# A transformer kernel whose split products read their moving columns with the two halves interleaved

## The chip, the cores and the metric

The kernel runs on one core of a Trainium2 chip. The metric is the device time of one execution in microseconds. Five engines work side by side and wait for one another by semaphores: PE multiplies matrices, DVE and ACT do elementwise work, POOL a little of it, and SP issues most transfers from the chip's main memory. PE reads both operands from the on-chip memory SBUF and adds its output into PSUM, a second on-chip memory, which DVE and ACT read ("evacuate").

## The reference

Two small transformer stacks of two layers each run one after the other over 256 tokens of width 1024, in float32. Cut to what matters:

```python
# first stack                                     # second stack
x = x + fox_mixer(rms_norm(x), ...)               x = x + gla_mixer(rmsnorm(x), ...)
x = x + square(relu(h @ w_up)) @ w_down           x = x + (silu(a) * u) @ w_down   # a, u: conv of h @ w_up
x = x + mla_mixer(h, ...)                         x = x + (b * conv(c * u)) @ w_out
x = x + square(relu(h @ w_up)) @ w_down           x = x + (silu(a) * u) @ w_down
x = rms_norm(x)                                   return rmsnorm(x)
```

The mixers are two kinds of causal softmax attention (Fox, MLA), a gated linear attention (GLA) and a short convolution. Nearly all arithmetic is in the products `h @ w` with a weight of 1024 or more rows.

## The kernel before

The tokens lie in two blocks of 128. A product of activations and weights is done in **split** form: ACT rounds a float32 operand to the format fp32r (the high part, `wh` for weights, `hh` for activations), DVE subtracts it from the original (the low part, `wl`, `hl`), and PE adds three products, high by high, high by low and low by high. In PE's terms each has a stationary operand of 128 columns, loaded anew each time, and a moving one whose columns stream through. In the trace a product reads `out<-moving,stationary`.

There are four kinds of split product. `proj` and `accum` hold an activation block and move 512 weight columns (384 or 320 in MLA); `mm3` issues the three. `proj_T` holds 128 weight columns and moves the activations of all 256 tokens, so its output is transposed; two such outputs share one PSUM tile. `proj_wide` moves 528 columns as twice 264. `accum_by_token` does the last products of the program token block by token block, the last ones in pieces of 256 columns. The moving columns are read in running order and land in PSUM in running order. The other products (attention scores and their use, transposes, the first two rounds of the program on unsplit data, `plain`) are ordinary float32.

Weights come by transfers into `raw` tiles (four), are split into `wh` and `wl` (five of each) and used in the order of a plan written out ahead. Output tiles are PSUM banks: four `acc`, three `up`, one `tp`. Elementwise work that follows a product is put into a queue and issued some steps later (`after`, with a table of delays, `DLY`); attention and GLA's core run as generators that put a step between the products (`side`). The order of the instructions on each engine is set when the program is built; at run time each engine takes its own in order and waits only where data is missing.

What the change touches: `mm` (line 339) issues every product; `by_row` (lines 399 and 401) multiplies a transposed output by a row of factors per token; `scaled` (line 591) multiplies by a factor per token on ACT; `scaled_wide` does so for the two tiles of `proj_wide`; `add_x` (lines 579 and 581) adds an output to x; and the evacuations of the ffn (line 616), of GLA's gate (line 1223) and of the short convolution (lines 1435 and 1447).

Of the kernel before, what the change touches and what calls it, by code (L numbers as in the profile page):

```python
# [18 lines left out]
P = 128  # L19
# [141 lines left out]
class Builder:  # L161
# [176 lines left out]
    def mm(self, out, lhsT, rhs, start, stop):  # L338
        self.nc.tensor.matmul(out, lhsT, rhs, start=start, stop=stop, skip_group_check=True)  # L339

    def mm3(self, ps, h, u, kk, n, start, stop):
        hh, hl = h
        wh, wl = u.hi[:, kk, :n], u.lo[:, kk, :n]
        self.mm(ps, hh, wh, start, False)
        self.mm(ps, hh, wl, False, False)
        self.mm(ps, hl, wh, False, stop)

    def up_tile(self):
        return self.up_p.tile([P, 512], F32, tag="up", name=self.name("up"))
# [10 lines left out]
    def proj(self, h, nk, n, evac, tiles=None, k0=0):  # L360

        ps = tiles or [self.up_tile(), self.up_tile()]
        k = k0
        while k < nk:
            u = self.unit()
            for kk in range(u.kn):
                for t in range(2):
                    self.mm3(ps[t][:, :n], h.get(t, k), u, kk, n, k == 0, k == nk - 1)
                    if k == nk - 1:
                        evac(t, ps[t])  # L370
                    self.tick()
                k += 1

    def proj_T(self, h, nk, evac, tile_fn=None):


        ps = [(tile_fn or self.up_tile)() for _ in range(2)]
        k = 0
        while k < nk:
            u = self.unit()  # L380
            for kk in range(u.kn):
                hh, hl = h.both(k)
                for f in range(4):
                    o = ps[f // 2][:, f % 2 * S:f % 2 * S + S]
                    wh, wl = [x[:, kk, f * P:(f + 1) * P] for x in (u.hi, u.lo)]
                    self.mm(o, wh, hh, k == 0 and f % 2 == 0, False)
                    self.mm(o, wl, hh, False, False)
                    self.mm(o, wh, hl, False, k == nk - 1)
                    if f % 2:
                        if k == nk - 1:  # L390
                            evac(f // 2, ps[f // 2])
                        self.tick()
                k += 1

    def by_row(self, out, ps, row, mul=None):

        r = lambda x: x.rearrange("p (i s) -> p i s", i=2)
        if mul is None:
            self.nc.vector.tensor_tensor(out=r(out), in0=r(ps), in1=row, op=ALU.mult)
        else:  # L400
            self.nc.vector.scalar_tensor_tensor(out=r(out), in0=r(ps), scalar=mul, in1=row, op0=ALU.mult, op1=ALU.mult)  # L401

    def proj_wide(self, h, evac, tile_fn):

        ps = [(tile_fn(), self.acc_tile()) for _ in range(2)]
        n = WIDE // 2
        for k in range(8):
            if k % 2 == 0:
                u = self.unit()
            for t in range(2):  # L410
                hh, hl = h.get(t, k)
                for i in range(2):
                    o = ps[t][i][:, :n]
                    wh, wl = [x[:, k % 2, i * n:i * n + n] for x in (u.hi, u.lo)]
                    self.mm(o, hh, wh, k == 0, False)
                    self.mm(o, hh, wl, False, False)
                    self.mm(o, hl, wh, False, k == 7)
                if k == 7:
                    evac(t, *ps[t])
                self.tick()  # L420

    def scaled_wide(self, out, a, b, col):

        n = WIDE // 2
        self.scaled(out[:, 0:n], a[:, 0:n], col)
        self.scaled(out[:, n:512], b[:, 0:512 - n], col)
        return b[:, 512 - n:n]

    def accum(self, acc, h, ks, first, last, done=None, cs=(0, 1)):

        for c in cs:
            k = 0
            while k < len(ks):
                u = self.unit()
                for kk in range(u.kn):
                    for t in range(2):
                        self.mm3(acc[t][c], h.get(t, ks[k]), u, kk, 512, first and k == 0, last and k == len(ks) - 1)
                        if last and k == len(ks) - 1:
                            done(t, c, acc[t][c])
                        self.tick()  # L440
                    k += 1

    def accum_by_token(self, acc, h, ks, done):

        us = [self.unit(), self.unit()]
        n = len(ks)
        xs = self.x[1][1]
        self.nc.vector.tensor_tensor(out=xs, in0=acc[1][1], in1=xs, op=ALU.add)
        for t in range(2):
            for c in range(2):  # L450
                if not (t and c):
                    for i, k in enumerate(ks):
                        self.mm3(acc[t][c], h.get(t, k), us[c], i, 512, False, i == n - 1)
                        self.tick()
                    done(t, c, acc[t][c], 0)
                    continue
                for o in (0, 256):
                    ps = self.up_tile()[:, 0:256]
                    for i, k in enumerate(ks):
                        hh, hl = h.get(t, k)  # L460
                        wh, wl = [x[:, i, o:o + 256] for x in (us[c].hi, us[c].lo)]
                        self.mm(ps, hh, wh, i == 0, False)
                        self.mm(ps, hh, wl, False, False)
                        self.mm(ps, hl, wh, False, i == n - 1)
                        self.tick()
                    done(t, c, ps, o)

    def new_acc(self):

# [103 lines left out]
    def add_x(self, hook, scale=None):  # L573
        nc = self.nc

        def done(t, c, ps, o=None):
            xs = self.x[t][c] if o is None else self.x[t][c][:, o:o + ps.shape[1]]
            if scale is None:
                nc.vector.tensor_tensor(out=xs, in0=ps, in1=xs, op=ALU.add)
            else:  # L580
                nc.vector.scalar_tensor_tensor(out=xs, in0=ps, scalar=scale[:, t:t + 1], in1=xs, op0=ALU.mult, op1=ALU.add)
            if o is None:
                hook(t, c)
            else:
                hook(t, c, xs, o)

        return done

    def scaled(self, out, ps, col):

        self.nc.scalar.activation(out=out, in_=ps, func=AF.Copy, scale=col)


# [13 lines left out]
    def ffn1(self, h, rs, hook):  # L607
# [4 lines left out]
        def evac(j):  # L612
            def f(b, ps):
                r = self.tmp_tile()
                sq = self.tmp_tile()
                nc.scalar.activation(out=r, in_=ps, func=AF.Relu)

                def square():
                    nc.vector.tensor_tensor(out=sq, in0=r, in1=r, op=ALU.mult)
                    self.after(DLY[4], lambda: self.split_pair(sq, hid, 4 * j + 2 * b))  # L620

                self.after(DLY[3], square)
            return f
# [344 lines left out]
    def mla(self, h, rs, hook):  # L968
# [20 lines left out]

        def ev_kv(t, ps):  # L990
            c = self.tmp_tile()
            self.scaled(c[:, :256], ps[:, :256], rs[:, t:t + 1])
            self.scaled(kc[:, t * 64:(t + 1) * 64], ps[:, 256:320], rs[:, t:t + 1])
            self.after(DLY[7], lambda: self.prep(c[:, :256], t, [0, 1], [(ckv, self.vec("kva"))], self.acc_tile))
            self.after(DLY[8], lambda: stat(t, c, 0, 256, 1.0 / 256))
            if t:
# [24 lines left out]

        def ev_q(t, ps):
            c = self.tmp_tile()
            self.scaled(c[:, :384], ps[:, :384], rs[:, t:t + 1])
            self.after(DLY[11], lambda: self.prep(c[:, :384], t, [0, 1, 2], [(cq, self.vec("qa"))], self.acc_tile))
            self.after(DLY[12], lambda: stat(t, c, 1, 384, 1.0 / 384))
            if t:
                self.after(DLY[12] + 6, lambda: rs2.make_row(2))
# [97 lines left out]
    def gla(self, h, rs, hook):  # L1126
# [93 lines left out]
        def ev_g(i):  # L1220
            def f(t, ps):
                gs = self.tmp_tile()
                nc.scalar.activation(out=gs, in_=ps, func=AF.Silu, scale=rs[:, t:t + 1])

                def gain():
                    nc.vector.tensor_tensor(out=gs, in0=gs, in1=hg[:, i * 512:(i + 1) * 512], op=ALU.mult)
# [195 lines left out]
    def sc(self, h, rs, hook):  # L1422
# [9 lines left out]
        def ev_u(i):  # L1432
            def f(b, ps):
                z = cs.pop(b)
                nc.vector.tensor_tensor(out=z, in0=ps, in1=z, op=ALU.mult)

                def go():
                    cv[b] = self.tmp_tile()
                    self.conv_pair(cv[b], z, cw, 4 * i + 2 * b)

                self.after(DLY[25 + b], go)
            return f

        def ev_b(i):
            def f(b, ps):
                c = cv.pop(b)
                nc.vector.tensor_tensor(out=c, in0=ps, in1=c, op=ALU.mult)
                self.after(DLY[29], lambda: self.split_pair(c, y, 4 * i + 2 * b))
            return f

# [94 lines left out]
    def start(self, h, stat):  # L1545
# [25 lines left out]
            return r  # L1571

        def plain(t, k):
            self.mm(ps[t], hg[t, 0][:, k * P:(k + 1) * P], self.raws[0][:, k], k == 0, False)

        with self.tc.manual_schedule():

# [150 lines left out]
```

## Time and profile before

| | |
|---|---|
| median of 3 runs | 1157.27 us (1157.15 to 1157.37) |
| the profiled execution's own time | 1156.24 us |
| its span, first to last instruction | 1154.5 us |
| PE busy | 1142.0 us in 7769 instructions |
| weight loads | 1030.1 us, beside PE |
| DVE busy | 804.8 us in 1196 |
| ACT busy | 610.9 us in 923 |
| mean granted TensorE clock | 0.999 |
| moved from main memory | 204.97 MB, 178 GB/s |

The page's busy share of PE says only that PE always has a product under way: products overlap, so a product that is shown with 280 ns may stand 117 ns after the one before. How fast PE runs is therefore read from the starts of products (the timeline) or from a piece of the chain of waits that holds many products in a row. Idle time stands behind a group's busy time, with what ended it.

### The profile page before, as it was taken

Reading aid. Unit: us, or ns where it says so; the run is one execution under the profiler, and the core shown is the slowest. Engines: PE = TensorE matmul, PEld = TensorE weight load, DVE = VectorE, ACT = ScalarE, POOL = GpSimd, SP = SyncE. Lnnn points to the kernel's source line nnn. Section 1 sums busy time; section 2 is a strip of 40 time slices with the busy share of each in tenths; the row PEclk is TensorE's granted clock in tenths of the full one; section 3 lists DMA queues with packets and bytes.
Section 4 is the critical chain, followed back from the end, with each engine's and each line's share of the span. In section 5 each row is a group of like instructions: output and inputs, shape, how many; then the busy total and the mean of one; then the engine's idle time right before and its main releaser. Section 6 shows DMA issues by size and latency. Waiting matters only on the chain.

```text
span 1154.5 us, 19192 instructions
## 1 busy us (share of the span) xinstructions
PE 1142.0 (99%) x7769; PEld 1030.1 (89%) x7769; DVE 804.8 (70%) x1196; ACT 610.9 (53%) x923; POOL 33.2 (3%) x55
## 2 busy tenths in 40 slices
PE   8999999999999999999999999999999999999997
PEld 6987998998888999899898789999989999999996
DVE  6686755555686755555788569777786668887775
ACT  5465554445665545444563556455555446555453
POOL 0000100000000100000010000000001000000001
PEclk9999999999999999999999999999999999999999
DMA  9744455555463556555555355556665564656551
GB/s 341 276 146 146 160 197 191 183 183 167 135 203 120 168 192 195 192 184 183 185 178 170 110 165 164 180 179 191 200 217 185 194 185 134 196 175 213 183 159 62
DMA packets 137802, 207.30 MB, mean 180 GB/s; under 512 B 10529, under 2 KB 65009, under 8 KB 137713
## 3 DMA queue, kind: packets, MB, share of 16 engines
q1 hardware_dynamic: 136576, 203.89, 55.1%
q10 hardware_dynamic: 1136, 2.17, 0.5%
q8 instruction: 61, 1.00, 0.4%
q14 instruction: 29, 0.23, 0.1%
HBM read 204.97 MB, written 1.07 MB: 178 GB/s over the span
## 4 chain that ended last, share of the span: by engine, by line
PE 92%; DVE 5%; ACT 2%; issue 1%; POOL 0%; ACTq 0%; DVEq 0%; POOLq 0%
PE up L339 52%; PE acc L339 37%; DVE wl L312 1%; PE acc L502 1%; ACT p L672 1%; DVE p L691 1%; PE tp L502 1%; ACT wh L294 0%; DVE p L682 0%; ACT junk L535 0%; PE tp L512 0%; DVE kT L1207 0%; PE acc L1582 0%; DVE pT L700 0%; DVE bias L758 0%
## 5 line engine op out<-in xcount | busy, mean ns | idle before, releaser
L312 DVE TENSOR_TENSOR wl<-raw,wh 128x1024 fp32r<-128x1024 f32 (+2 forms) x373 | 454.1, 1219 | 261.4 <-ACT wh L294 259.5
L294 ACT CAST wh<-raw 128x1024 fp32r<-128x1024 f32 (+2 forms) x373 | 389.5, 1045 | 432.3 <-PE up L339 278.2
L339 PE MATMUL up<-hh,wh 128*128 128x256 f32 x1564 | 439.2, 281 | 0.0
L339 PE MATMUL up<-hh,wl 128*128 128x256 f32 x1564 | 437.7, 280 | 0.0
L339 PE MATMUL up<-hl,wh 128*128 128x256 f32 x1564 | 436.5, 280 | 0.0
L339 PEld LDWEIGHTS up<-hh,wh 128*128 128x128 f32 x1564 | 294.3, 188 | 3.0 <-issue 1.5
L339 PEld LDWEIGHTS up<-hh,wl 128*128 128x128 f32 x1564 | 294.1, 188 | 1.5
L339 PEld LDWEIGHTS up<-hl,wh 128*128 128x128 f32 x1564 | 294.2, 188 | 0.3 <-DVE hl L491 0.2
L339 PE MATMUL acc<-wh,hh 128*128 128x512 f32 (+1 forms) x606 | 235.8, 389 | 0.2 <-DVE mx L691 0.2
L339 PE MATMUL acc<-wh,hl 128*128 128x512 f32 (+1 forms) x606 | 233.3, 385 | 0.0
L339 PE MATMUL acc<-wl,hh 128*128 128x512 f32 (+1 forms) x606 | 232.8, 384 | 0.0
L339 PEld LDWEIGHTS acc<-wh,hl 128*128 128x128 f32 x606 | 113.8, 188 | 24.5 <-DVE hl L708 0.3
L339 PEld LDWEIGHTS acc<-wh,hh 128*128 128x128 f32 x606 | 113.8, 188 | 23.1 <-DVE mx L691 0.6
L339 PEld LDWEIGHTS acc<-wl,hh 128*128 128x128 f32 x606 | 113.9, 188 | 21.6
L1340 DVE SCALAR_TENSOR_TENSOR tmp<-tmp,vecs,tmp 128x255 f32<-128x255 f32 x192 | 78.0, 479 | 18.0 <-ACT tmp L1338 18.0
L339 PE MATMUL up<-wh,hh 128*128 128x512 f32 (+4 forms) x142 | 53.9, 382 | 0.3 <-DVE tmp L401 0.3
L339 PE MATMUL up<-wl,hh 128*128 128x512 f32 (+4 forms) x142 | 51.6, 364 | 1.3 <-DVE wl L312 1.3
L339 PE MATMUL up<-wh,hl 128*128 128x512 f32 (+4 forms) x142 | 51.4, 364 | 0.0
L1338 ACT ACTIVATE tmp<-tmp,vecs 128x256 f32<-128x256 f32 x96 | 40.9, 497 | 0.0
L1349 DVE TENSOR_TENSOR hl<-tmp,hh 128x512 fp32r<-128x512 f32 x58 | 38.2, 685 | 0.0
L1348 ACT CAST hh<-tmp 128x512 fp32r<-128x512 f32 x58 | 34.2, 622 | 2.2 <-DVE tmp L1393 2.2
L339 PEld LDWEIGHTS up<-wh,hh 128*128 128x128 f32 x142 | 26.7, 188 | 7.5 <-issue 3.4
(205 smaller groups left out, 770.5 us busy)
## 6 DMA issues: line engine op xcount, KB each, us to landing
raw<-ffn_w_up SPq DMA_DIRECT2D x176, 256.0 KB, 4.1
raw<-ffn_w_up SPq DMA_DIRECT2D x32, 1024.0 KB, 5.4
raw<-ffn_w_down SPq DMA_DIRECT2D x32, 1024.0 KB, 5.0
raw<-ffn_w_down SPq DMA_DIRECT2D x44, 512.0 KB, 6.5
raw<-sc_w_in SPq DMA_DIRECT2D x12, 1024.0 KB, 5.2
raw<-fox_w_in SPq DMA_DIRECT2D x10, 1024.0 KB, 9.4
raw<-gla_w_in SPq DMA_DIRECT2D x10, 1024.0 KB, 5.1
raw<-fox_w_out SPq DMA_DIRECT2D x4, 1024.0 KB, 5.0
```

What stands on the lines that cost most here:

```text
L294: self.last_hi = nc.scalar.copy(hi[:, :kn, :w], self.raws[r][:, k:k + kn])
L312: self.last_wl = nc.vector.tensor_tensor(out=u.lo[:, :kn, :w], in0=self.raws[r][:, k:k + kn], in1=u.hi[:, :kn, :w].bitcast(F32), op=ALU.su ...
L339: self.nc.tensor.matmul(out, lhsT, rhs, start=start, stop=stop, skip_group_check=True)
L502: self.nc.tensor.transpose(tp[:, i * P:(i + 1) * P], src[:, i * P:(i + 1) * P], self.ident)
L672: self.nc.scalar.activation(out=p[:, o:o + n], in_=p[:, o:o + n], func=AF.Exp, scale=scale, bias=nm[:, j:j + 1], accum_out=sm[:, j:j + 1])
L691: self.nc.vector.tensor_tensor_reduce(out=p[:, o:o + n], in0=lgs[h][:, w], in1=bias(h)[:, w], scale=1.0, scalar=NEG, op0=ALU.add, op1=ALU. ...
L1338: nc.scalar.activation(out=out, in_=z, func=AF.Copy, scale=w[:, 2:3])
L1340: nc.vector.scalar_tensor_tensor(out=out[:, d:], in0=z[:, :S - d], scalar=w[:, 2 - d:3 - d], in1=out[:, d:], op0=ALU.mult, op1=ALU.add)
L1348: nc.scalar.copy(hi, src)
L1349: nc.vector.tensor_tensor(out=lo, in0=src, in1=hi.bitcast(F32), op=ALU.subtract)
```

## The change

A split product's moving operand is read as first column of the left half, first of the right half, second of the left, second of the right, and so on. The output is still written to PSUM in running order, so PSUM holds the columns interleaved. Each evacuation reads PSUM at every second element, the left half first and then the right, and so puts the columns back in order. `plain` shares its PSUM tiles with split products and is done the same way. [...] In MLA, the evacuation of the KV projection copies all 320 columns where it copied 256.

```diff
+    def mmw(self, out, lhsT, rhs, start, stop):
+        self.mm(out.rearrange("p (b a) -> p b a", a=2), lhsT, rhs.rearrange("p (a b) -> p b a", a=2), start, stop)
+
+    def woven(ps, n=1):
+        return ps.rearrange("p (b a) -> p a b", a=2) if n == 1 else ps.rearrange("p (i b a) -> p i a b", i=n, a=2)
+
+    def like(x, ps):
+        if len(x.shape) == 3:
+            return x.rearrange("p i (a b) -> p i a b", a=2)
+        return x.rearrange("p (a b) -> p a b", a=2) if len(ps.shape) == 3 else x.rearrange("p (i a b) -> p i a b", i=ps.shape[1], a=2)
+
     def mm3(self, ps, h, u, kk, n, start, stop):
-        self.mm(ps, hh, wh, start, False)
-        self.mm(ps, hh, wl, False, False)
-        self.mm(ps, hl, wh, False, stop)
+        self.mmw(ps, hh, wh, start, False)
+        self.mmw(ps, hh, wl, False, False)
+        self.mmw(ps, hl, wh, False, stop)
...
-                        evac(t, ps[t])
+                        evac(t, self.woven(ps[t][:, :n]))
...
-                            evac(f // 2, ps[f // 2])
+                            evac(f // 2, self.woven(ps[f // 2], 2))
...
-            self.nc.vector.tensor_tensor(out=r(out), in0=r(ps), in1=row, op=ALU.mult)
+            self.nc.vector.tensor_tensor(out=out, in0=ps, in1=row, op=ALU.mult)
         else:
-            self.nc.vector.scalar_tensor_tensor(out=r(out), in0=r(ps), scalar=mul, in1=row, op0=ALU.mult, op1=ALU.mult)
+            for i in range(2):
+                self.nc.vector.scalar_tensor_tensor(out=out[:, i], in0=ps[:, i], scalar=mul, in1=row[:, i], op0=ALU.mult, op1=ALU.mult)
...
-        self.scaled(out[:, 0:n], a[:, 0:n], col)
-        self.scaled(out[:, n:512], b[:, 0:512 - n], col)
-        return b[:, 512 - n:n]
+        m = n // 2
+        self.scaled(out[:, 0:n], a, col)
+        self.scaled(out[:, n:n + m], b[:, 0], col)
+        self.scaled(out[:, n + m:512], b[:, 1, :m - 16], col)
+        return b[:, 1, m - 16:]
...
-            self.scaled(c[:, :256], ps[:, :256], rs[:, t:t + 1])
-            self.scaled(kc[:, t * 64:(t + 1) * 64], ps[:, 256:320], rs[:, t:t + 1])
+            self.scaled(c[:, :320], ps, rs[:, t:t + 1])
+            self.scaled(kc[:, t * 64:(t + 1) * 64], ps[:, 1, 96:160], rs[:, t:t + 1])
```

On PE nothing moves but one group of four small products in GLA's core, which changes places with its neighbours; SP and POOL keep their order. Two places on ACT and DVE show what moves there. On ACT, in Fox, the evacuation of V after `proj_wide` stood as follows (`v` is the result, `acc` the output tiles, `wh` the next weights).

```order
L294 CAST wh_400<-raw_243 128x2x512
L591 ACTIVATE v_207<-acc_296,rs_117 128x264
L591 ACTIVATE v_207<-acc_297,rs_117 128x248
L591 ACTIVATE v_207<-acc_298,rs_117 128x264
L591 ACTIVATE v_207<-acc_299,rs_117 128x248
L294 CAST wh_452<-raw_253 128x2x512
```

After the change it is this.

```order
L294 CAST wh_400<-raw_243 128x2x512
L615 ACTIVATE v_207<-acc_296,rs_117 128x264
L615 ACTIVATE v_207<-acc_297,rs_117 128x132
L615 ACTIVATE v_207<-acc_297,rs_117 128x116
L615 ACTIVATE v_207<-acc_298,rs_117 128x264
L615 ACTIVATE v_207<-acc_299,rs_117 128x132
L615 ACTIVATE v_207<-acc_299,rs_117 128x116
L294 CAST wh_454<-raw_253 128x2x512
```

The two pieces of 248 columns have become two each, ahead of the next weights' rounding; GLA has the same. On DVE, in Fox's attention, a stretch with one evacuation of Q (`qT`), a step of the softmax (`nm`, `rc`) and the low part of the next weights (`wl`) was this.

```order
L401 SCALAR_TENSOR_TENSOR qT_204<-up_587,rowb_217 128x512
L769 SCALAR_TENSOR_TENSOR nm_732<-mx_727,ctok 128x4
L679 RECIPROCAL rc_761<-sm_674 128x4
L312 TENSOR_TENSOR wl_750<-raw_530,wh_749 128x2x512
L770 TENSOR_TENSOR nm_732<-nm_732,ctok 128x4
```

And it becomes this.

```order
L419 SCALAR_TENSOR_TENSOR qT_204<-up_589,rowb_217 128x256
L793 SCALAR_TENSOR_TENSOR nm_735<-mx_730,ctok 128x4
L419 SCALAR_TENSOR_TENSOR qT_204<-up_589,rowb_217 128x256
L794 TENSOR_TENSOR nm_735<-nm_735,ctok 128x4
L703 RECIPROCAL rc_765<-sm_676 128x4
L312 TENSOR_TENSOR wl_754<-raw_532,wh_753 128x2x512
```

The evacuation is in two halves with a small softmax step between them, and `nm`'s second step now stands ahead of the weights' low part; some of the rows behind, up to 30 further on, change places with their neighbours.

## Rows read from the trace of the kernel before

**Rows 1.** The page's part 1: busy us (share of the span) and instructions.
```profile
PE 1142.0 (99%) x7769; PEld 1030.1 (89%) x7769; DVE 804.8 (70%) x1196; ACT 610.9 (53%) x923; POOL 33.2 (3%) x55
```

**Rows 2.** What PE waited for: us in total, times, longest; first and last of six.
```profile
PE acc L1582 <- POOL ident masks.py:199: 1.3, 1, 1.3
...
PE acc L339 <- DVE mx L691: 0.2, 1, 0.2
```

**Rows 3.** The chain that ended last, pieces: start us, us, what.
```profile
147.58 11.09 PE acc L339 x48
...
876.05 60.95 PE up L339 x521
...
967.95 27.32 PE up L339 x233
```

**Rows 4.** Split products by form: names, stationary, moving, count; busy us, mean ns; idle before.
```profile
L339 PE MATMUL up<-hh,wh 128*128 128x256 f32 x1564 | 439.2, 281 | 0.0
...
L339 PE MATMUL acc<-wh,hh 128*128 128x512 f32 x558 | 222.1, 398 | 0.2 <-DVE mx L691 0.2
...
L339 PE MATMUL up<-wh,hh 128*128 128x512 f32 x90 | 37.4, 419 | 0.3 <-DVE tmp L401 0.3
...
L339 PE MATMUL acc<-wh,hh 128*128 128x264 f32 x48 | 13.7, 286 | 0.0
...
L339 PE MATMUL acc<-hh,wh 128*128 128x256 f32 x44 | 12.3, 280 | 0.0
...
L339 PE MATMUL up<-wh,hh 128*128 128x384 f32 x16 | 5.6, 348 | 0.0
...
L339 PE MATMUL up<-wh,hh 128*128 128x320 f32 x16 | 5.2, 326 | 0.0
...
L339 PE MATMUL up<-wh,hh 128*128 128x264 f32 x16 | 4.6, 290 | 0.0
...
L339 PE MATMUL up<-wh,hh 128*128 128x256 f32 x4 | 1.1, 282 | 0.0
```

**Rows 5.** Stretches: us, busy us (count) by engine, granted clock, DMA share, GB/s.
```profile
147.58:169.89 22.31, 22.31 (x145) 20.23 (x145) 12.28 (x13) 10.51 (x12) 0.00 (x0) 1.00 0.57 189
967.95:995.27 27.32, 27.32 (x235) 27.32 (x234) 23.52 (x35) 15.28 (x23) 0.00 (x0) 1.00 0.48 149
876.05:937.00 60.95, 60.95 (x522) 60.95 (x522) 40.72 (x51) 26.70 (x33) 0.00 (x0) 1.00 0.57 186
```

**Rows 6.** Timeline of PE, 600 to 603 us: start us, us, product; twelve apart.
```profile
600.18 0.28 PE L339 MATMUL acc<-hh,wh 128*128 128x256 f32 x1
...
601.54 0.29 PE L339 MATMUL acc<-hh,wh 128*128 128x256 f32 x1
...
602.97 0.28 PE L339 MATMUL acc<-hh,wh 128*128 128x256 f32 x1
```

**Rows 7.** Plain f32 on PE: timeline from 6 us, and the transposes' group.
```profile
5.71 0.59 PE L339 MATMUL up<-raw,tmp 128*128 128x512 f32 x1
6.14 0.60 PE L502 MATMUL acc<-ident,x 128*128 128x128 f32 x4
...
L502 PE MATMUL acc<-ident,x 128*128 128x128 f32 x112 | 17.3, 281 | 0.0
```

**Rows 8.** Evacuations on DVE and ACT by form.
```profile
L399 DVE TENSOR_TENSOR tmp<-up,rowb 128x512 f32<-128x512 f32 x48 | 31.0, 684 | 0.0
...
L579 DVE TENSOR_TENSOR x<-acc,x 128x512 f32<-128x512 f32 x19 | 12.3, 683 | 0.7 <-PE acc L339 0.7
...
L581 DVE SCALAR_TENSOR_TENSOR x<-acc,rs,x 128x512 f32<-128x512 f32 x12 | 8.6, 746 | 0.6 <-PE acc L339 0.6
...
L1317 DVE SCALAR_TENSOR_TENSOR tmp<-acc,hr,tmp 128x256 f32<-128x256 f32 x8 | 3.4, 477 | 0.1
...
L591 ACT ACTIVATE v<-acc,rs 128x248 f32<-128x248 f32 x4 | 1.9, 466 | 0.0
```

**Rows 9.** The chain between 60 and 100 us, by line.
```profile
by line: ACT p L672 21.9%; DVE p L691 17.4%; DVE wl L312 17.0%; DVE p L682 12.2%; PE acc L339 7.6%; issue 5.9%; DVE pT L700 5.8%; DVE hl L708 3.3%; DVE rc L679 2.6%; DVE nm L769 2.3%; DVE nm L770 2.1%; PE up L339 2.0%; DVE qT L401 1.7%; DVE
```

More of the change, by code (lines that the diff above doesn't have):

```diff
@@ L339, in mm @@
         self.nc.tensor.matmul(out, lhsT, rhs, start=start, stop=stop, skip_group_check=True)
+    def mmw(self, out, lhsT, rhs, start, stop):
+        self.mm(out.rearrange("p (b a) -> p b a", a=2), lhsT, rhs.rearrange("p (a b) -> p b a", a=2), start, stop)
+    @staticmethod
+    def woven(ps, n=1):
+        return ps.rearrange("p (b a) -> p a b", a=2) if n == 1 else ps.rearrange("p (i b a) -> p i a b", i=n, a=2)
+    @staticmethod
+    def like(x, ps):
+        if len(x.shape) == 3:
+            return x.rearrange("p i (a b) -> p i a b", a=2)
+        return x.rearrange("p (a b) -> p a b", a=2) if len(ps.shape) == 3 else x.rearrange("p (i a b) -> p i a b", i=ps.shape[1], a=2)
     def mm3(self, ps, h, u, kk, n, start, stop):
@@ L385, in proj_T @@
                     wh, wl = [x[:, kk, f * P:(f + 1) * P] for x in (u.hi, u.lo)]
-                    self.mm(o, wh, hh, k == 0 and f % 2 == 0, False)
-                    self.mm(o, wl, hh, False, False)
-                    self.mm(o, wh, hl, False, k == nk - 1)
+                    self.mmw(o, wh, hh, k == 0 and f % 2 == 0, False)
+                    self.mmw(o, wl, hh, False, False)
+                    self.mmw(o, wh, hl, False, k == nk - 1)
                     if f % 2:
                         if k == nk - 1:
-                            evac(f // 2, ps[f // 2])
+                            evac(f // 2, self.woven(ps[f // 2], 2))
                         self.tick()
@@ L395, in by_row @@
     def by_row(self, out, ps, row, mul=None):
-        r = lambda x: x.rearrange("p (i s) -> p i s", i=2)
+        out, row = self.like(out, ps), self.like(row, ps)
         if mul is None:
-            self.nc.vector.tensor_tensor(out=r(out), in0=r(ps), in1=row, op=ALU.mult)
+            self.nc.vector.tensor_tensor(out=out, in0=ps, in1=row, op=ALU.mult)
         else:
-            self.nc.vector.scalar_tensor_tensor(out=r(out), in0=r(ps), scalar=mul, in1=row, op0=ALU.mult, op1=ALU.mult)
+            for i in range(2):
+                self.nc.vector.scalar_tensor_tensor(out=out[:, i], in0=ps[:, i], scalar=mul, in1=row[:, i], op0=ALU.mult, op1=ALU.mult)
     def proj_wide(self, h, evac, tile_fn):
@@ L414, in proj_wide @@
                     wh, wl = [x[:, k % 2, i * n:i * n + n] for x in (u.hi, u.lo)]
-                    self.mm(o, hh, wh, k == 0, False)
-                    self.mm(o, hh, wl, False, False)
-                    self.mm(o, hl, wh, False, k == 7)
+                    self.mmw(o, hh, wh, k == 0, False)
+                    self.mmw(o, hh, wl, False, False)
+                    self.mmw(o, hl, wh, False, k == 7)
                 if k == 7:
-                    evac(t, *ps[t])
+                    evac(t, *[self.woven(x[:, :n]) for x in ps[t]])
                 self.tick()
@@ L438, in accum @@
                         if last and k == len(ks) - 1:
-                            done(t, c, acc[t][c])
+                            done(t, c, self.woven(acc[t][c]))
                         self.tick()
@@ L447, in accum_by_token @@
         xs = self.x[1][1]
-        self.nc.vector.tensor_tensor(out=xs, in0=acc[1][1], in1=xs, op=ALU.add)
+        ps = self.woven(acc[1][1])
+        self.nc.vector.tensor_tensor(out=self.like(xs, ps), in0=ps, in1=self.like(xs, ps), op=ALU.add)
         for t in range(2):
@@ L454, in accum_by_token @@
                         self.tick()
-                    done(t, c, acc[t][c], 0)
+                    done(t, c, self.woven(acc[t][c]), 0)
                     continue
@@ L461, in accum_by_token @@
                         wh, wl = [x[:, i, o:o + 256] for x in (us[c].hi, us[c].lo)]
-                        self.mm(ps, hh, wh, i == 0, False)
-                        self.mm(ps, hh, wl, False, False)
-                        self.mm(ps, hl, wh, False, i == n - 1)
+                        self.mmw(ps, hh, wh, i == 0, False)
+                        self.mmw(ps, hh, wl, False, False)
+                        self.mmw(ps, hl, wh, False, i == n - 1)
                         self.tick()
-                    done(t, c, ps, o)
+                    done(t, c, self.woven(ps), o)
     def new_acc(self):
@@ L576, in done @@
         def done(t, c, ps, o=None):
-            xs = self.x[t][c] if o is None else self.x[t][c][:, o:o + ps.shape[1]]
+            xs = self.x[t][c] if o is None else self.x[t][c][:, o:o + ps.shape[1] * ps.shape[2]]
+            x3 = self.like(xs, ps)
             if scale is None:
-                nc.vector.tensor_tensor(out=xs, in0=ps, in1=xs, op=ALU.add)
+                nc.vector.tensor_tensor(out=x3, in0=ps, in1=x3, op=ALU.add)
             else:
-                nc.vector.scalar_tensor_tensor(out=xs, in0=ps, scalar=scale[:, t:t + 1], in1=xs, op0=ALU.mult, op1=ALU.add)
+                nc.vector.scalar_tensor_tensor(out=x3, in0=ps, scalar=scale[:, t:t + 1], in1=x3, op0=ALU.mult, op1=ALU.add)
             if o is None:
@@ L589, in scaled @@
     def scaled(self, out, ps, col):
+        if len(ps.shape) > 2:
+            out = self.like(out, ps)
         self.nc.scalar.activation(out=out, in_=ps, func=AF.Copy, scale=col)
@@ L615, in f @@
                 sq = self.tmp_tile()
-                nc.scalar.activation(out=r, in_=ps, func=AF.Relu)
+                nc.scalar.activation(out=self.like(r, ps), in_=ps, func=AF.Relu)
                 def square():
@@ L1023, in ev_q @@
             c = self.tmp_tile()
-            self.scaled(c[:, :384], ps[:, :384], rs[:, t:t + 1])
+            self.scaled(c[:, :384], ps, rs[:, t:t + 1])
             self.after(DLY[11], lambda: self.prep(c[:, :384], t, [0, 1, 2], [(cq, self.vec("qa"))], self.acc_tile))
@@ L1222, in f @@
                 gs = self.tmp_tile()
-                nc.scalar.activation(out=gs, in_=ps, func=AF.Silu, scale=rs[:, t:t + 1])
+                nc.scalar.activation(out=self.like(gs, ps), in_=ps, func=AF.Silu, scale=rs[:, t:t + 1])
                 def gain():
@@ L1434, in f @@
                 z = cs.pop(b)
-                nc.vector.tensor_tensor(out=z, in0=ps, in1=z, op=ALU.mult)
+                nc.vector.tensor_tensor(out=self.like(z, ps), in0=ps, in1=self.like(z, ps), op=ALU.mult)
                 def go():
@@ L1446, in f @@
                 c = cv.pop(b)
-                nc.vector.tensor_tensor(out=c, in0=ps, in1=c, op=ALU.mult)
+                nc.vector.tensor_tensor(out=self.like(c, ps), in0=ps, in1=self.like(c, ps), op=ALU.mult)
                 self.after(DLY[29], lambda: self.split_pair(c, y, 4 * i + 2 * b))
@@ L1573, in plain @@
         def plain(t, k):
-            self.mm(ps[t], hg[t, 0][:, k * P:(k + 1) * P], self.raws[0][:, k], k == 0, False)
+            self.mmw(ps[t], hg[t, 0][:, k * P:(k + 1) * P], self.raws[0][:, k], k == 0, False)
         with self.tc.manual_schedule():
```

## The prediction

> **What bounds the kernel now.** I read the page's busy shares first: PE is busy 1142.0 of 1154.5 us, DVE 804.8, ACT 610.9 [rows 1]. PE's own waits come next: six of them, from 1.3 us down to 0.2 [rows 2]. So nothing keeps PE from its work, and the time is the sum of the distances from one product to the next. A product's own duration does not give that distance, since products overlap (a 128x256 one is shown as 280 ns). The chain of waits does: 48 products of 512 columns take 11.09 us, 231.0 ns each, and 521 of 256 columns take 60.95 us, 117.0 ns each [rows 3]. A straight line through both is 3.0 ns a product and 0.4453 ns a column ((231.0 - 117.0) / 256). The granted clock of those stretches is 1.00, the 2.4 GHz level [rows 5], which is 0.4167 ns a column. So every moving column costs 0.0286 ns, 6.9%, more than the clock asks.
>
> Where does this excess come from? Not from the other engines: 521 products of 256 columns are 117.0 ns apart in a stretch with DVE busy 40.72 of 60.95 us, and 233 of them 117.3 ns (27.32 / 233) where DVE is busy 23.52 of 27.32 [rows 3, 5]. It does change from place to place inside one stretch: twelve products from 600.18 to 601.54 are 113.3 ns apart, the next twelve, to 602.97, 119.2 [rows 6], with the same shape, clock and instruction; what differs is where the operands lie. And it is missing where PE takes 4-byte columns more slowly: plain f32 transposes run at 107 ns per 128 columns ((0.60 - 0.28) / 3), 0.83 ns a column, which is two clock periods with nothing on top [rows 7]. An excess per column, that depends on addresses and shows only at one 4-byte column per clock period, looks like the read of the moving operand that does not quite keep up.
>
> **The change part by part.** (1) Every split product gets another order of its moving columns: first column of the left half, first of the right half, second of the left, and so on. Instructions, weight loads, columns and the order on PE stay as they were, except four products of the GLA core that move by two places; the output is written to PSUM in running order as before. The split products by form [rows 4] are 3 x (1564 + 44 + 4) = 4836 of 256 columns, 3 x (558 + 90) = 1944 of 512, 3 x (48 + 16) = 192 of 264, 48 of 320 and 48 of 384: 2,317,824 columns. At 0.4453 ns and 3.0 ns a product they hold 1032 + 21 = 1053 us of the span, so any change of rate is the whole result. The trace has no product with interleaved columns. Bounds: at best the excess goes, 0.4167 ns a column, -0.0286 x 2,317,824 = **-66 us**; a little better still if part of the 3.0 ns goes too, but a pair of weight load and product was never closer than the transposes' 107 ns, which for the 256-column products allows 4836 x 10 = 48 us and, with 216 ns for the 512-column ones, 1944 x 15 = 29 us: -77 us. At worst the interleaved read runs like the f32 one, 0.8333 ns a column: (0.8333 - 0.4453) x 2,317,824 = **+899 us**. Neither end is near; I take the excess as gone, since the only excess in the trace is one of consecutive columns at full rate, and interleaving gives each place in memory two periods between its columns, the spacing at which the f32 rows show none. I keep the other end as a rival.
>
> [...]
>
> (2) The evacuations read PSUM at every second element. Their number hardly changes, and a full tile takes DVE 683 to 746 ns (line 399, the adds of lines 579 and 581) [rows 8]. Whether the step costs anything no row shows: bounds are nothing and twice the time. [...] The cover is PE's supply of work: a stage with three `up` tiles lets a tile wait. If the time doubled, a stretch like 967.95 to 995.27 with some six evacuations would have DVE at 23.52 + 4.1 = 27.6 us, more than PE's 25.6 after the gain, which is 2 us there and 4 with its twin near 700; and the 31 adds into x (19 and 12) could delay the norm behind them, 31 x 0.68 = 21 us if all were exposed.
>
> (3) Four evacuations by row with a factor (2 of line 401 in Fox, 2 in GLA) become two instructions of 128x256: a 256-wide one of this kind takes 477 ns [rows 8], so 2 x 477 - 684 = +270 ns each, 1.1 us on DVE. Four ACT pieces of 248 columns (466 ns) become 132 and 116; a second instruction is at most another 466 ns, 1.9 us in all. Both stand before weight splits in their queues, which PE gets through buffers five deep; I count them as 1 us. The two KV evacuations that grow by 64 columns are too little to count.
>
> (4) What is late next. In Fox's attention, from 60 to 100 us, the chain that ends last is DVE's and ACT's softmax work, not PE's products (lines 672, 691, 682 and 312 hold two thirds of it) [rows 9]. PE there cannot finish earlier by its own speed alone. The gain is 66 of 1154 us, 5.7%; for these 40 us that is 2.3 us that may stay out, and I allow as much again for MLA's attention, which is built alike: 4 of the 4.6.
>
> Sum, made against the profiled execution (1156.24 us: its span of 1154.5 and 1.7 around it, 1.0 under the median of 1157.27): 1156.24 - 66 + 1 + 4 = 1095; with the 1.0 to the median, **1096 us**.
>
> **The rivals.**
> - *Half the gain.* The interleaved read is not free of the excess but settles at the better of the two spacings of [rows 6]: 256-column products at 113.3 in place of 117.0, 4836 x 3.7 = 18 us, the others by the same share, 1944 x 7.3 = 14 us: -32, 1125 us. For it: that spacing is in the trace. Against: it still lies above the clock, and interleaving changes the very access order.
> - *Nothing.* The excess belongs to the weight load or the write into PSUM, which keep their addresses; 1157 us and the microsecond of (3), 1158. For it: each weight load stands at its product's start and is reloaded every time. Against: the excess grows with the moving columns, and a 512-column product loads no more weights than a 256-column one.
> - *The evacuations are exposed.* No change on PE, and the step in PSUM doubles the 31 adds: up to 1157 + 21 = 1178 us. It decides once an add is so late that the transposes behind it, which PE has next, wait. Against: none of PE's six waits of today is longer than 1.3 us.
> - *Half rate.* The interleaved columns are taken at 0.8333 ns: 1157 + 899 = **2056 us**, much slower. It decides in every split product, whatever else happens. For it: PE does read 4-byte columns at that rate in all f32 products of the trace (0.43 us for 512, from 5.71 to 6.14) [rows 7]. Against: those are consecutive columns too, so their rate belongs to the number format and not to the order, and the split products read the same 4 bytes at nearly twice that rate. [...]
>
> **How the numbers follow.** My forecast, 1080 to 1112 us, has 0.47; half the gain 0.16, nothing 0.11 (0.08 of it within 0.2%, about what a measurement of this kernel can tell from no change; 0.03 above), exposed evacuations 0.07, half rate 0.19. Faster is 0.47 + 0.16 = 0.63, same 0.08, slower 0.03 + 0.07 + 0.19 = 0.29. The range leaves out half rate and so runs from 1080 (1157 - 77) to 1178; by itself the likeliest case has 1080 to 1112.
>
> **What would show it.** In the chain of waits after, 48 products of 512 columns should take about 10.4 us (216 ns each) and 96 of 256 columns about 10.6 (110 each), PE still almost without waits; the f32 transposes should stay at 107 ns. Step (2) is right if line 399's evacuation keeps 684 ns; step (4) if the stretch between 60 and 100 us shrinks by less than the ffn stages. If 512-column products stand at 231 ns, my reading of the excess is wrong; at about 430 ns, each column waits for its own access, and the forecast fails altogether.

## The result

The changed kernel takes 1106.15 us (median of 4 runs, 1105.91 to 1106.69) where the kernel before takes 1157.24: a ratio of 0.9559 with a 95% interval of 0.9543 to 0.9576, 51.1 us less. The forecast was 1096, the range 1080 to 1178. One of the six executions of the last version below (v1) took 2895.18 us, for a reason that no run shows, and is left out of its numbers.

The page's part 1 of the kernel after, against [rows 1]:

```profile
PE 1087.8 (98%) x7769; PEld 1004.0 (91%) x7769; DVE 801.4 (73%) x1200; ACT 609.4 (55%) x927; POOL 29.6 (3%) x55
```

PE has as many products as before, and DVE and ACT do nearly the same work (801.4 and 609.4 us where they did 804.8 and 610.9). The busy shares look alike and hide the gain, which stands in the chain of waits of the kernel after (start us, us, what), against [rows 3]:

```profile
144.34 10.36 PE acc L339 x48
154.70 10.72 PE up L339 x96
...
839.45 58.45 PE up L339 x521
...
927.29 26.18 PE up L339 x233
```

48 products of 512 columns take 10.36 us, 215.8 ns each in place of 231.0; 96 of 256 columns take 10.72 us, 111.7 ns in place of 117.0 (521 of them: 112.2). In the timeline of the kernel after, 36 products of 384 columns start 162.5 ns apart from 295.08 to 300.77 us, and 23 of 320 columns 135.8 ns apart from 303.06 to 306.05, both at a granted clock of 1.00. From 320 to 512 columns that is (215.8 - 135.8) / 192 = 0.4167 ns a column, 2.4 columns a ns. The spread from place to place that [rows 6] showed is gone with it: in the ffn stages before, 96 products took from 11.21 to 11.35 us, for example

```profile
491.89 11.21 PE up L339 x96
514.21 11.35 PE up L339 x96
```

and in the kernel after, every such piece takes 10.72. The granted clock of these stretches is still 1.00: the windows view of the kernel after (us, busy us and count by engine, granted clock, DMA share, GB/s), against [rows 5]:

```profile
144.34:165.42 21.08, 21.08 (x145) 19.79 (x145) 12.28 (x13) 10.50 (x12) 0.00 (x0) 1.00 0.59 200
839.45:897.90 58.45, 58.45 (x522) 58.28 (x522) 40.36 (x51) 26.73 (x33) 0.00 (x0) 1.00 0.59 192
```

The same transfers, splits and evacuations stand in a shorter stretch, with DVE at 12.28 us as before and transfers at 200 in place of 189 GB/s. PE's waits in the kernel after, against [rows 2]:

```profile
PE up L339 <- DVE tmp L419: 1.7, 1, 1.7
PE acc L1606 <- POOL ident masks.py:199: 1.3, 1, 1.3
PE up L339 <- DVE wl L312: 1.3, 1, 1.3
PE tp L523 <- DVE tmp L144: 1.0, 1, 1.0
PE tp L533 <- DVE pT L724: 0.6, 1, 0.6
PE up L339 <- DVE pT L724: 0.5, 1, 0.5
PE acc L523 <- DVE tmp L144: 0.4, 1, 0.4
PE tp L533 <- DVE p L706: 0.3, 1, 0.3
PE acc L339 <- issue: 0.2, 1, 0.2
PE acc L339 <- DVE mx L715: 0.2, 1, 0.2
```

They add up to 7.5 us where the six of before added up to 4.2. The largest new one is GLA's evacuation of Q, 1.7 us (0.3 before); three more are for the softmax's probabilities (`p`, `pT`): a faster PE reaches work of DVE that is not ready. The evacuations by form in the kernel after, against [rows 8]:

```profile
L416 DVE TENSOR_TENSOR tmp<-up,rowb 128x512 f32<-128x512 f32 x48 | 30.8, 682 | 0.0
...
L601 DVE TENSOR_TENSOR x<-acc,x 128x512 f32<-128x512 f32 x19 | 12.3, 683 | 0.6 <-PE acc L339 0.6
L603 DVE SCALAR_TENSOR_TENSOR x<-acc,rs,x 128x512 f32<-128x512 f32 x12 | 8.5, 745 | 0.3 <-PE acc L339 0.2
...
L419 DVE SCALAR_TENSOR_TENSOR qT<-up,rowb 128x256 f32<-128x256 f32 x4 | 1.6, 417 | 0.0
```

Reading PSUM at every second element cost these evacuations nothing: 682, 683 and 745 ns where it was 684, 683 and 746.

Where the gain lies by stage is read from the starts of the long pieces in the two chains. First the kernel before:

```profile
125.39 22.18 PE up L339 x188
...
281.67 18.01 PE acc L339 x78
...
391.61 22.17 PE up L339 x188
...
547.87 18.01 PE acc L339 x78
...
689.03 27.32 PE up L339 x233
```

And the kernel after:

```profile
123.25 21.09 PE up L339 x188
...
270.82 16.84 PE acc L339 x78
...
377.13 21.09 PE up L339 x188
...
524.70 16.84 PE acc L339 x78
...
661.56 26.18 PE up L339 x233
```

| stage | before, us | after, us | gain | split products closer by, us |
|---|---|---|---|---|
| start and Fox (0 to the first ffn) | 125.4 | 123.3 | 2.1 (1.7%) | 4.8 |
| first ffn (to the end of the x78 piece) | 174.3 | 164.4 | 9.9 (5.7%) | 9.9 |
| MLA | 91.9 | 89.5 | 2.5 (2.7%) | 3.3 |
| second ffn | 174.3 | 164.4 | 9.9 (5.7%) | 9.9 |
| GLA | 123.2 | 120.0 | 3.1 (2.5%) | 6.0 |
| the rest (conv ffns, short convolution, end) | 465.5 | 442.8 | 22.6 (4.9%) | 23.1 |

The last column lays the two timelines of PE side by side, product by product: it adds up how much closer each split product's successor starts in the kernel after. Distances above 0.4 us in either kernel hold a wait and are left out of it. Its sum is 57.0 us, of which 50.1 reach the span. The ffn stages keep all of it; the start, Fox, MLA and GLA give back 6.4 us to longer waits of PE, to slower f32 products at the start and to other products.

### The profile page after: what moved, and what is told of

Its sections match the earlier page's. It is cut to its first block, busy times and chain, and to the rows that moved or that the text cites. A ratio compares the mean times of both kernels' runs of the same rounds, so it can differ in the third digit from the quotient of the medians.

```text
span 1104.4 us, 19202 instructions
## 1 busy us (share of the span) xinstructions
PE 1087.8 (98%) x7769; PEld 1004.0 (91%) x7769; DVE 801.4 (73%) x1200; ACT 609.4 (55%) x927; POOL 29.6 (3%) x55
## 4 chain that ended last, share of the span: by engine, by line
PE 87%; DVE 7%; ACT 3%; issue 1%; DMA 1%; POOL 0%; SPq 0%; ACTq 0%; DVEq 0%; POOLq 0%
PE up L339 51%; PE acc L339 33%; DVE wl L312 2%; PE acc L523 1%; ACT wh L294 1%; DMA bias<-rows 1%; PE tp L523 1%; ACT p L696 1%; DVE p L715 1%; DVE x L601 0%; DVE p L706 0%; PE tp L533 0%; DVE tmp L1364 0%; ACT junk L556 0%; PE acc L1606 0%
## 5 line engine op out<-in xcount | busy, mean ns | idle before, releaser
L339 PE MATMUL up<-hh,wh 128*128 128x256 f32 x1564 | 431.8, 276 | 0.0
L339 PE MATMUL up<-hh,wl 128*128 128x256 f32 x1564 | 430.1, 275 | 0.0
L339 PE MATMUL up<-hl,wh 128*128 128x256 f32 x1564 | 429.4, 275 | 0.0
L339 PEld LDWEIGHTS up<-hh,wh 128*128 128x128 f32 x1564 | 300.1, 192 | 3.0 <-issue 1.5
L339 PEld LDWEIGHTS up<-hh,wl 128*128 128x128 f32 x1564 | 300.1, 192 | 0.9
L339 PEld LDWEIGHTS up<-hl,wh 128*128 128x128 f32 x1564 | 299.8, 192 | 0.3 <-DVE hl L512 0.2
L339 PE MATMUL acc<-wh,hh 128*128 128x512 f32 (+1 forms) x606 | 227.4, 375 | 0.2 <-DVE mx L715 0.2
L339 PE MATMUL acc<-wh,hl 128*128 128x512 f32 (+1 forms) x606 | 225.0, 371 | 0.1
L339 PE MATMUL acc<-wl,hh 128*128 128x512 f32 (+1 forms) x606 | 224.8, 371 | 0.0
```

## The experiments

The theory: the whole gain is PE's reading of the moving operand, whose consecutive columns now lie in different places of SBUF. The rivals: the other parts of the change (strided evacuations, split instructions) also move the time; any two-dimensional access pattern would do it; the distance has to be large. Most kernels below start from the kernel before and change only the order in which the moving columns are read; their evacuations are those of before.

**e1_read_only: the read alone.** The interleaved read for split products, everything else as before.

```diff
+    def mmx(self, out, lhsT, rhs, start, stop):
+        self.mm(out.rearrange("p (b a) -> p b a", a=2), lhsT, rhs.rearrange("p (a b) -> p b a", a=2), start, stop)
```

> The kernel before, with the split products' moving columns interleaved as in the change, but the first f32 products and every evacuation left in running order (so the columns of the output are in the wrong places). Theory (the order of the moving read is the whole gain): 512-column products 216 ns apart and 256-column ones 112 as in the kernel after, time 1103 to 1107 us. Rival (the strided PSUM evacuations or other edits cost or gain something): more than 3 us away from the 1106 us of the kernel after.

Measured: 1105.38 us, ratio 0.9555 (0.9539 to 0.9571), and the products stand as far apart as in the kernel after:

```profile
398.15 10.36 PE acc L339 x48
408.51 10.72 PE up L339 x96
```

The read order is the whole gain. The kernel after took 0.6 to 0.8 us more (1105.99 and 1106.15), but on other chips, and the intervals of the ratios overlap; the rest of the change costs no more than about that. GLA's new wait stands here too, where no evacuation is split or strided, so the faster products alone bring it:

```profile
PE up L339 <- DVE tmp L404: 1.6, 1, 1.6
```

**e3_not_T: one kind of product alone.** As e1, but `proj_T` issues its products by `mm`.

> As the run before, but the transposed projections (the 1612 x 3 products of 256 columns) keep the running order. Theory (each product's gain is its own and the parts add up): the 512-column products gain 15.2 ns each, 1944 x 15.2 = 30 us, the other forms about 2: 1157 - 32 = 1125 us, the 256-column ones still 117 ns apart. Rival (the excess comes from neighbouring instructions disturbing one another): the 256-column products change too, or the time is outside 1120 to 1130.

Measured: 1129.38 us, ratio 0.9763 (0.9748 to 0.9777). The time is inside the stated interval but 4 us above the theory's own figure. Its chain of waits:

```profile
404.54 10.36 PE acc L339 x48
414.90 11.19 PE up L339 x96
```

The 512-column products have all of their gain, and the 256-column ones, 11.19 / 96 = 116.6 ns, none. Product by product as above, the 512-column ones are 29.3 us closer than before (29.4 in the kernel after) and the 256-column ones 0.9 us further apart: each product's gain is its own. All split products together are 30.9 us closer; 27.5 reach the time. Most of the 4 us that the theory missed is lost in the start, Fox, MLA and GLA (3.7 us of the span), where the kernel after loses too.

**d2, d4, d8, d16: how far apart.** What the expectations call a line is a piece of 16 bytes, four columns. The order is 0, d, 1, d + 1 and so on in pieces of 2d columns of 4 bytes; d is the only change from one run to the next (the 264-column products keep d = 132 where 2d does not divide them).

```diff
+        n = rhs.shape[1]
+        d = 4 if n % 8 == 0 else n // 2
+        self.mm(out.rearrange("p (c b a) -> p c b a", a=2, b=d), lhsT,
+                rhs.rearrange("p (c a b) -> p c b a", a=2, b=d), start, stop)
```

> The kernel before with moving columns in the order 0, 2, 1, 3, 4, 6, 5, 7 and so on: consecutive columns are 8 bytes apart instead of 4 (output columns in the wrong places). Theory (the excess comes of consecutive columns in the same small piece of memory, and columns must lie further apart): no or little gain, 1145 to 1160 us. Rival (any two-dimensional pattern switches the reader to another way of working): the full gain, 1103 to 1107 us. [...]

> The kernel before with consecutive moving columns 64 bytes apart: 0, 16, 1, 17, and so on in pieces of 32 columns (the 264-column products with their halves interleaved; output columns in the wrong places). Theory (two neighbouring places a line or more apart are enough): the full gain, 1103 to 1107 us. Rival (the halves must lie in memory parts that are half a kilobyte or more apart): no gain, 1150 to 1160 us. [...]

> The kernel before with consecutive moving columns 16 bytes apart: 0, 4, 1, 5, 2, 6, 3, 7 and so on (output columns in the wrong places). 8 bytes gave nothing and 64 bytes everything. Theory A (the memory is read in pieces of 16 bytes, and two columns after one another must come from different pieces): full gain, 1104 to 1107 us. Theory B (pieces or alternating parts of 32 or 64 bytes): no gain or half of it, 1130 to 1158 us.

> As the run before with 32 bytes between consecutive columns: 0, 8, 1, 9, and so on. Theory A: full gain, 1104 to 1107 us. Theory B with pieces of 32 bytes: full gain here and none at 16 bytes; with pieces of 64 bytes: none here either, 1150 to 1158 us.

| bytes between consecutive columns | us | ratio (95%) |
|---|---|---|
| 4 (before) | 1156.85; beside d4 and d8 1156.76 | |
| 8 (d2) | 1156.77 | 0.9999 (0.9990 to 1.0009) |
| 16 (d4) | 1105.42 | 0.9555 (0.9541 to 0.9569) |
| 32 (d8) | 1105.57 | 0.9555 (0.9541 to 0.9570) |
| 64 (d16) | 1105.64 | 0.9557 (0.9543 to 0.9572) |
| half the operand, 512 to 1024 (e1) | 1105.38 | 0.9555 (0.9539 to 0.9571) |

The chain of waits of d2:

```profile
147.70 11.09 PE acc L339 x48
158.78 11.22 PE up L339 x96
```

And of d4:

```profile
398.12 10.36 PE acc L339 x48
408.49 10.72 PE up L339 x96
```

All or nothing, with the step between 8 and 16 bytes: d2 has the same kind of access pattern as d4 and gains nothing (1156.77 us), so it is not the pattern. In these runs the gain comes where two columns after one another lie in different pieces of 16 bytes (1105.42 us); more distance brings nothing (1105.57 and 1105.64 us).

**m4_step: another piece each time.** The same 16 bytes between consecutive columns, but in one direction (0, 4, 8, ...), so that a piece is used again only after all the others.

```diff
+        self.mm(out.rearrange("p (b a) -> p b a", b=4), lhsT, rhs.rearrange("p (a b) -> p b a", b=4), start, stop)
```

> The kernel before with the moving columns in steps of four: 0, 4, 8, and so on to the end, then 1, 5, 9 (output columns in the wrong places): consecutive columns are 16 bytes apart as in d4, but no piece of 16 bytes is read again before all others have been. Theory A (two consecutive columns must come from different pieces, each read by itself): full gain, 1104 to 1107 us. Theory C (two pieces are held and each gives its four columns in turn, so a piece must be used again at once): slower, towards 0.83 ns a column, up to 2000 us.

Measured: 2193.75 us, ratio 1.8966 (1.8935 to 1.8998). Its chain:

```profile
251.64 22.14 PE acc L339 x48
273.78 22.39 PE up L339 x96
```

512 columns take 461 ns and 256 take 233: 0.89 ns a column, more than the 0.83 of the f32 products. Theory A fell and theory C came out. This is the rival of half rate, in another order than the change's: 2194 us where the prediction worked out 2056. So it is not enough that neighbours come from different pieces; as far as these orders show, each piece must also be used again soon. With d4 two pieces take turns and each gives its four columns within eight. How many pieces could take turns no run shows.

**e4_stationary, e5_half_load, e6_stationary2: why 111.7 and not 109.** At the 0.4167 ns a column that the kernel after shows from 320 to 512 columns, 512 columns are 213.3 ns and 256 are 106.7; it needs 2.5 ns more with 512 and 5.0 ns more with 256. The suspect is the weight load beside each product. All three start from e1 and change the stationary operand of `proj_T`.

```diff
-                    wh, wl = [x[:, kk, f * P:(f + 1) * P] for x in (u.hi, u.lo)]
+                    wh, wl = [x[:, kk, f:512:4] for x in (u.hi, u.lo)]                                        # e4
+                    wh, wl = [x[:, kk, f // 2 * 256 + f % 2:f // 2 * 256 + 256:2] for x in (u.hi, u.lo)]      # e6
+                    if k: o, wh, wl = o[0:64], wh[:, 0:64], wl[:, 0:64]                                       # e5
```

> The interleaved read of e1, and in the transposed projections the stationary operand takes every fourth column of 512 (16 bytes apart) in place of 128 neighbouring ones (outputs in the wrong places). The 256-column products stand 111.7 ns apart, 2.5 ns more than the 109.2 that the clock and the floor of the longer ones give (512: 215.8 = 213.3 + 2.5). Theory (the weight load beside them is their limit and its read has the excess that the moving read had): 256-column products go to 109 ns, 4800 x 2.5 = 12 us less than e1, 1093 us. Rival 1 (the load is the limit but not its order): 111.7, 1105 us. [...]

> The interleaved read of e1, and in the transposed projections only 64 of the 128 stationary columns are loaded and multiplied after the first step over the contraction (half of that output is left out). Theory (the weight load is what holds the 256-column products at 111.7 ns): with half the load they go to 109.2 ns or less, about 7/8 x 4836 x 2.5 = 10 us less than e1, 1095 us. Rival (a cost of the 256-column product itself): still 111.7 ns, 1105 us.

> The interleaved read of e1, and in the transposed projections the stationary operand takes every second column of 256 (8 bytes apart; outputs in the wrong places). With 16 bytes between its columns the load took about twice as long, and with half the columns the 256-column products came down to 109 ns. Theory (the load of neighbouring columns carries the excess of the moving read, and 8 bytes are as little as they were there): 111.7 ns, 1105 us. Rival 1 (any spread within a line helps the load): 109 ns, 1094 us. Rival 2 (the load wants four columns of a line): slower, above 1110 us.

Measured: 1691.31 (ratio 1.4621, 1.4596 to 1.4645), 1096.54 (0.9481, 0.9467 to 0.9495) and 1137.00 us (0.9830, 0.9815 to 0.9844). The 256-column pieces of the three chains, e4 first:

```profile
211.02 22.50 PE up L339 x96
```

e5:

```profile
406.13 10.51 PE up L339 x96
```

e6:

```profile
156.97 11.40 PE up L339 x96
```

With half the load the products come to 109.5 ns and the kernel gains 8.8 us more, as the theory said. In e4 and e6 the load's order is the only change to these products, and it lengthens the pair, so a load can be the limit. That it is the load which holds them at 111.7 rests on e5 alone, where each product also writes only 64 rows of its output; a limit in that write is not ruled out. My theory that another spread would help the load as it helps the moving read fell, and so did the one that 8 bytes would change nothing: at 8 bytes between the load's columns a pair takes longer (118.8 ns), at 16 bytes twice as long (234 ns). Two pieces taking turns were not tried for the load.

**v1: two mendings.** In the kernel after the f32 products at the start read interleaved columns too, so that they fit into their shared tile. Timeline of PE, kernel after:

```profile
7.12 3.50 PE L339 MATMUL up<-raw,tmp 128*128 128x512 f32 x6
```

And in v1, where they read in running order and write PSUM at every second element:

```profile
7.27 2.93 PE L339 MATMUL up<-raw,tmp 128*128 128x512 f32 x6
```

```diff
-            self.mmw(ps[t], hg[t, 0][:, k * P:(k + 1) * P], self.raws[0][:, k], k == 0, False)
+            self.mm(ps[t].rearrange("p (b a) -> p a b", a=2), hg[t, 0][:, k * P:(k + 1) * P],
+                    self.raws[0][:, k].rearrange("p (a b) -> p a b", a=2), k == 0, False)
...
-            self.by_row(tk, ps, rs.row(0), 128.0 ** -0.5)
+            self.by_row(tk, ps, rs.row(0))
...
-                nc.vector.tensor_tensor(out=half(E, b), in0=tk, in1=half(E, b), op=ALU.mult)
+                nc.vector.scalar_tensor_tensor(out=half(E, b), in0=tk, scalar=128.0 ** -0.5, in1=half(E, b), op0=ALU.mult, op1=ALU.mult)
```

> The kernel after with two mendings: the f32 products at the start read their columns in running order again and write them to PSUM at every second element (so their tile still holds what the split products expect), and GLA's factor for Q is multiplied in with the gate, so that its evacuation is one instruction again. Theory (the interleaved read costs the f32 passes 540 in place of 430 ns, and the start waits for them): 8 passes x 0.11 = 0.9 us less than the kernel after, 1105.2 us. Rival (the start waits for transfers, and the strided write costs the same): 1106 us.

> The kernel after, for comparison on the same chip: 1105.5 to 1106.5 us.

Measured: v1 1105.16 us (1104.93 to 1105.39), ratio 0.9552 (0.9540 to 0.9565), against 1105.99 (1105.93 to 1106.27) for the kernel after on the same chip. v1 is 0.83 us faster, the two sets of runs do not overlap, and 3.50 - 2.93 = 0.57 us of it stands in the rows above. The two mendings were not run apart, but GLA's wait hardly shrank, so its second instruction was not what made it:

```profile
PE up L339 <- DVE tmp L416: 1.6, 1, 1.6
```

Why interleaved columns slow the f32 products, when they speed up the split ones, stays open.

## Why the prediction was right

**The reading of the excess** was right: 0.0286 ns a column belonged to the read of the moving operand, and with another order it went. The 0.4167 ns a column that the sum sets against it stands in no row of the kernel before; the kernel after shows it, in the products of 320 to 512 columns at a granted clock of 1.00. The 512-column products came out at 215.8 ns where I had worked out 216, and e1 shows that the read order alone gives the whole gain.

**The reason I gave for the new order** was only half of one. I argued that interleaving gives each place in memory two periods between its columns, as in the f32 rows. By that, m4, which leaves each piece alone for much longer, should have gained as well, and it takes nearly twice the time; and the f32 products, which were to show that this spacing is free of loss, become slower when they are interleaved. That the chosen order has two pieces taking turns, which is what the runs show to count, was not in my working, and to that extent it was luck.

**The size** was 10 us too large, and the mis-sized term is that of the 256-column products: I let them drop by 0.0286 x 256 = 7.3 ns to 110 and took the f32 transposes' 107 ns as the floor of a pair of weight load and product. But 107 ns is the time of the transposes' own 128 moving columns at 0.83 ns, and says little about the load. The split pair stops at 111.7 ns, with half the load at 109.5 (e5). So they gained 5.3 ns in place of 7.3, 4836 x 2.0 = 10 us less.

The other terms came out nearly. The 66 us of (1) were 57.0 when measured product by product: 25.1 from the 256-column products (35.4 in my sum), 29.4 from the 512-column ones (28.5) and 2.5 from the rest (2.4). Of these, 6.9 us did not reach the span, where I had allowed 1 + 4 = 5.

**What is late next** (4): I allowed 4 us for Fox and MLA, and they gave back 3.5 (8.1 closer, 4.6 gained). I had nothing for GLA, which gave back 2.9. The share of 5.7% that I used for the sizes is too high in these stages: at 5.7% start, Fox and MLA (217.3 us) would gain 12.4 us, but they hold so many other products that their split products could give 8.1 at most.

In Fox the chain between 58 and 98 us is still that of the softmax, against [rows 9]; the kernel after:

```profile
by line: ACT p L696 18.2%; DVE p L715 14.8%; DVE wl L312 14.1%; DVE p L706 10.6%; issue 9.7%; PE acc L339 8.9%; DVE pT L724 5.8%; DVE hl L732 3.3%; DVE bias L782 3.1%; DVE qT L419 2.7%; PE tp L533 2.6%; DVE nm L794 2.3%; DVE rc L703 2.1%; A
```

Its two ends in the kernel before:

```profile
58.93 1.13 DVE wl L312
...
96.26 3.04 PE acc L339 x12
```

And in the kernel after:

```profile
58.41 1.13 DVE wl L312
...
95.34 2.86 PE acc L339 x12
```

The stretch takes 37.33 us before and 36.93 after, 1.1% less, where the ffn stages lose 5.7%. Its split products are 1.1 us closer, and PE gives most of that back in waits (1.0 us): the stretch hangs on DVE and ACT, whose work did not get shorter. So step (4) was right in kind.

**The evacuations** (2) have no term in the sum, and rightly: 682 ns for 684. **The split instructions** (3) cost less than I had put: a 256-wide one with the row takes 417 ns, not 477, so 2 x 417 - 684 = 150 ns for each of four. What I had missed is that the f32 products at the start are interleaved too and lose by it (0.57 us in the rows above). The f32 transposes kept their distance, as expected (four in 0.60 us, before and after).

**The rivals.** Half the gain (1125), nothing (1158) and exposed evacuations (1178) are ruled out by e1 and the rows of line 416. Half rate and less came out in m4 (0.89 ns a column), but not for this order. My argument against it, that consecutive f32 columns also run at 0.83 ns and the order therefore has no part in it, was weak: the order of the columns alone takes the split products from 216 to 461 ns.

## What to carry to other kernels

A product's distance to the next, fitted over two lengths, splits into a fixed part and a price per column; if the price per column is high although PE waits for nothing (here 0.4453 ns, against half of the f32 products' 0.83), the operand's read order is worth a try. Here fp32r columns read from two 16-byte pieces in turn ran at 0.4167 ns a column (216 ns for 512), neighbours 7% slower (231 ns), and columns that do not return to a piece soon at less than half the rate (461 ns), so the pattern has to be measured and not only strided. Once the moving read runs at that rate, the weight load beside a 256-column product looks like the next limit (111.7 ns, 109.5 with half the load), and the straight line through two lengths no longer gives the price of a column: from 256 to 512 columns it would be 0.407 ns after the change, from 320 to 512 it is 0.4167. And a faster PE gains only where nothing else is late: the ffn stages kept all of it, the start, Fox, MLA and GLA little more than half (7.7 of 14.1 us).

## What the runs showed of the hardware

- Split (fp32r) products, 512 moving columns: 231.0 ns with neighbouring columns or 8 bytes apart, 215.8 with two pieces of 16 bytes in turn (16 bytes apart in d4, 1024 in the kernel after and e1; with 32 and 64 bytes, d8 and d16, the time is the same, 1105.57 and 1105.64 us), 461 with steps of 16 bytes in one direction (m4).
- Plain f32 passes went the other way: six products of 512 columns with interleaved halves took 3.50 us, in running order 2.93, in v1, which writes PSUM at every second element, as in the kernel before.
- A weight load of 128 columns beside a 256-column product: 111.7 ns a pair with neighbouring columns (e1), 118.8 with 8 bytes between them (e6), 234 with 16 bytes (e4); with 64 columns (and half of the output) 109.5 (e5).
- DVE read PSUM at every second element at the same speed: 682 ns for 128x512 against 684.
